# A hybrid decoder trunk: ten in place of six of layer 1's eleven up-projection pairs by seven products, in PSUM chains, with the sums of weights spread over more of the kernel and seven raw buffers

## The chip, the cores and the metric

The kernel runs on one core of one Trainium2 chip. The metric is device time in microseconds (us), the median of three runs. The core has five engines that work side by side: TensorE (PE, matrix products into the PSUM accumulators; its weight loads are listed as PEld), VectorE (DVE), ScalarE (ACT), GpSimd (POOL) and SyncE (SP, which here only issues transfers). Each takes its own instructions in the order in which they were laid down, and waits for others by semaphores.

## What is computed

Two decoder layers over a sequence of 512 rows and 1024 channels. Layer 0 is a causal convolution module, then a feed-forward block; layer 1 is windowed attention, then a feed-forward block; then a last norm. The part that matters here is the feed-forward block of layer 1:

```python
def swiglu_ffn(x, w_up, w_down):
    gate, up = jnp.split(x @ w_up, 2, axis=-1)
    return (jax.nn.silu(gate) * up) @ w_down

h = h + swiglu_ffn(rmsnorm(h, norm_ffn[l]), ffn_w_up[l], ffn_w_down[l])
```

`w_up` is 1024 x 5632 (gate and up), `w_down` is 2816 x 1024.

## The kernel before

**Three matmuls for one product.** A product in float32 accuracy is made of three in a shorter format: every operand is split into a high and a low part, and `mm3` (L352) issues high x high, high x low and low x high (L356 to L358). Weights arrive from memory in chunks of 128 x 1024 (512 KB): `load` (L244) issues the transfer on SP's queue into a tile `raw`, `split_weights` (L272) makes `whi` on ACT (L273) and `wlo` on DVE (L276). `advance` (L278) is called once for each chunk used. It loads up to `DMA_AHEAD` = 6 chunks ahead of the use and splits up to 3 ahead; there are four buffers each of `raw`, `whi` and `wlo`. `PLAN` (L105) is the order of all chunks.

**Pairs.** The 2816 hidden columns of layer 1 are 22 tiles, treated as eleven pairs 0 to 10. A step `("up", p)` computes gate and up of a pair for all 512 rows, a step `("low", p)` multiplies the pairs p and p+1 by their rows of `w_down` and adds to h. `STEPS1` (L32) gives the order: up 0, 1, 2, low 0, then up 3, 4, low 2; up 5, 6, low 4; up 7, 8, low 6; up 9, 10, low 8. Pair 10 is multiplied by its part of `w_down` at the very end, together with the last norm.

**Plain or by seven.** `plain_pair` (L742) uses four chunks and issues 96 matmuls of 512 columns into four PSUM banks. `seven_pair` (L773) cuts the product into 2 x 2 blocks and forms it from seven block products in place of eight (Strassen's scheme in Winograd's form). Each takes one chunk and 24 matmuls of 256 columns into a PSUM bank of its own. Three of the seven use a block of the weights as it is; the others use sums of blocks, S1 to S4. Their partners are blocks of the rows or sums of them, T1 to T4, made once by `Rows.sums` (L723) on POOL and split on ACT and DVE while pair 0 is computed. The results are combined in a tile `c` of four blocks c11 to c22: two copies on ACT (L788, L790), five operations on DVE (L792, L793, L797, L799, L801) and two on POOL (L794, L795). Then come the row scale, silu and the product of gate and up (L807 to L809). `SEVENS` (L57) lists the pairs by seven: 1, 3, 5, 6, 8, 9. So 0, 2, 4, 7 and 10 are plain. All five `low` steps are by seven, and there the products that share a result are added up in one bank already (`CHAINS`, L828): A11, S2, S3, A22 in chain x, S1 and S4 in z, A12 in y. A chain is read after each of its products. For these steps `forms_of` (L814) makes sums of the hidden values on POOL (L823) and splits them on ACT and DVE (L515 to L519).

**The order of the seven.** `SEVEN`, `SEVEN_FIRST` (for pair 1) and `SEVEN_LOW` give three orders; `order_of` picks one.

**Sums of weights.** `prepare` (L252) makes S1 to S4 of each step by seven in device memory: a transfer on SP's queue copies one block (L264), a transfer on POOL's queue adds the other (L268), three sums behind. It is a generator. `advance` takes one step of it at every chunk from the second part of layer 0's feed-forward block on, and it yields twice for a sum, so that a sum is made at every second chunk. The sums are then loaded like any chunk.

**What sets the order.** The kernel is written as a program in one order, and a scheduler lays it out engine by engine with a model of the times. A tile's buffer or PSUM bank (eight banks, L217) is given to a new tile when the last reader of the old one is done. Layer 0 works in two halves of the rows; its first half's projection and the conv of the second half run together. `Next` (L684) and `Rms` (L454) make the norm: squares on ACT, partial sums on POOL (L467), a product with ones on TensorE (L477), the power on POOL (L481), and a spread over the partitions on TensorE (L503). `flip` (L1422) transposes h between the products of pair 1.

Of the kernel before, what the change touches and what calls it, by code (L numbers as in the profile page):

```python
# [18 lines left out]
P = 128  # L19
# [46 lines left out]
def order_of(kind, pair):  # L66
    if kind == "low":
        return SEVEN_LOW
    return SEVEN_FIRST if pair == SEVENS[0] else SEVEN

# [8 lines left out]
def blocks_of(kind, pair):  # L79
    return [(kind, pair, n.split()[0]) for n in order_of(kind, pair)]  # L80

# [118 lines left out]
def hybrid_trunk(ctx: ExitStack, tc: tile.TileContext, xT, W, prm_in, wdw_in, sinks, relb, onehot, fin, lead, out):  # L200
# [33 lines left out]
    summed, preparing, loaded = {}, [iter(())], []  # L234

# [8 lines left out]
    def load(upto):  # L244
        while stream["dma"] < min(len(PLAN), upto):
            i = stream["dma"]
            r = wpool.tile([P, 1024], F32, tag="raw", name=uid("raw"), bufs=4)
            loaded[:] = [nc.sync.dma_start(r, chunk(PLAN[i])).ins]
            raws[i] = r
            stream["dma"] += 1  # L250

    def prepare():  # L252
# [7 lines left out]
        for c in adds + [None] * 3:  # L260
# [8 lines left out]
            yield  # L269
            yield  # L270

# [79 lines left out]

    def mm3(out, w, x, start, stop):  # L352
        if w[1] is None:
            nc.tensor.matmul(out, w[0], x, start=start, stop=stop)  # L354
            return
        nc.tensor.matmul(out, w[0], x[0], start=start, stop=False)  # L356
        nc.tensor.matmul(out, w[0], x[1], start=False, stop=False)  # L357
        nc.tensor.matmul(out, w[1], x[0], start=False, stop=stop)  # L358

# [39 lines left out]

    both = [wpool.tile([P, 1024], F32, tag="raw", name=uid("both"), bufs=4) for _ in range(KT // 2)]  # L400
    x_first = [both[k // 2][:, k % 2 * 512:k % 2 * 512 + 256] for k in range(KT)]
# [308 lines left out]
    class Rows:  # L710
# [12 lines left out]
        def sums(self):  # L723
# [49 lines left out]
    def seven_pair(pair, rows, pool, between=None):  # L773

        c = new_gates(pool)
        c11, c12, c21, c22 = (c[:, m, s] for m in range(2) for s in range(2))
        acc = {}
        for n, name in enumerate(order_of("up", pair)):
            w = [x.rearrange("p (a k c) -> p a k c", a=2, k=4) for x in get_seven("up", pair, n)]
            a, b = name.split()  # L780
            x = rows.block[b]
            r = acc[a] = bank().rearrange("p (a s) -> p a s", a=2)
            for which in range(2):
                for k in range(4):
                    mm3(r[:, which], [v[:, which, k, :] for v in w], [x[e][:, k, :] for e in range(2)],
                        which == 0 and k == 0, which == 1 and k == 3)
            if a == "A11":
                nc.scalar.copy(c11, r)  # L788
            elif a == "S1":
                nc.scalar.copy(c22, r)  # L790
            elif a == "S2":
                nc.vector.tensor_add(c12, r, c11)  # L792
                nc.vector.scalar_tensor_tensor(c21, acc["S3"], -1.0, c12, op0=ALU.mult, op1=ALU.subtract)  # L793
                nc.gpsimd.tensor_add(c12, c12, c22)  # L794
                nc.gpsimd.tensor_sub(c22, c21, c22)  # L795
            elif a == "A12":
                nc.vector.tensor_add(c11, r, c11)  # L797
# [36 lines left out]
    def low_pairs(pair, forms, rs):  # L834

        chains = {}
        for n, name in enumerate(order_of("low", pair)):
            whi, wlo = get_seven("low", pair, n)
# [380 lines left out]

    preparing[0] = prepare()  # L1220
    if True:
# [3 lines left out]
        rate[0] = 2  # L1225

        xkv = x["kv"]
        kq = quads.tile([P, 2, 512], F32, tag="quad", name="kq")
# [199 lines left out]

    forms, signed = {}, None
    for kind, pair in STEPS1:  # L1430
        if kind == "low":
# [77 lines left out]
```

## Time and profile before

| what | value |
|---|---|
| median of 3 runs | 1065.55 us (1065.12 to 1065.77) |
| the profiled execution's own time | 1065.14 us |
| its span, first to last instruction | 1062.6 us |
| mean granted TensorE clock | 0.998 |
| busy: PE / DVE / ACT / POOL | 99% / 70% / 52% / 41% |
| transfers | 187.92 MB, mean 177 GB/s |
| first matmul of pair 1 | 734.07 us |

The span leaves out some 2.5 us around the instructions. The busy share of TensorE counts the modelled ends of overlapping matmuls, so the distance from one start to the next is the better measure of what a matmul costs. In the rows of the profile L12 is line 12 of the kernel, "bank" is a PSUM bank, and the tile in front of the arrow is written, those behind it are read. In the views by time, the number in square brackets is how long the engine stood before the instruction, and for whom.

### The profile page before, as it was taken

Reading aid. Unit: us, or ns where it says so; the run is one execution under the profiler, and the core shown is the slowest. Engines: PE = TensorE matmul, PEld = TensorE weight load, DVE = VectorE, ACT = ScalarE, POOL = GpSimd, SP = SyncE. Lnnn points to the kernel's source line nnn. Section 1 sums busy time; section 2 is a strip of 40 time slices with the busy share of each in tenths; the row PEclk is TensorE's granted clock in tenths of the full one; section 3 lists DMA queues with packets and bytes.
Section 4 is the critical chain, followed back from the end, with each engine's and each line's share of the span. In section 5 each row is a group of like instructions: output and inputs, shape, how many; then the busy total and the mean of one; then the engine's idle time right before and its main releaser. Section 6 shows DMA issues by size and latency. Waiting matters only on the chain.

```text
span 1062.6 us, 16003 instructions
## 1 busy us (share of the span) xinstructions
PE 1051.8 (99%) x5878; PEld 914.9 (86%) x5878; DVE 748.1 (70%) x1159; ACT 554.1 (52%) x968; POOL 433.0 (41%) x523
## 2 busy tenths in 40 slices
PE   9999999999999999999999999999999999999996
PEld 8888889999988888888888877788989899898985
DVE  3999988977776644443437456677778779768867
ACT  3887888864655332322324455465634355444443
POOL 3999998810321311211213254305532415315401
PEclk9999999999999999999999999999999999999999
DMA  9238046576566787677775444466989665455532
GB/s 350 95 96 98 7 139 213 177 226 181 179 182 195 231 209 194 196 187 207 190 206 161 120 140 118 123 177 182 277 248 346 194 186 185 146 159 179 179 119 80
DMA packets 52058, 187.92 MB, mean 177 GB/s; under 512 B 6187, under 2 KB 12492, under 8 KB 51276
## 3 DMA queue, kind: packets, MB, share of 16 engines
q1 hardware_dynamic: 44924, 162.74, 47.5%
q0 software_dynamic: 6336, 23.07, 12.2%
q10 hardware_dynamic: 720, 1.10, 0.3%
q8 instruction: 46, 0.75, 0.3%
q14 instruction: 32, 0.26, 0.1%
HBM read 181.64 MB, written 51.38 MB: 219 GB/s over the span
## 4 chain that ended last, share of the span: by engine, by line
PE 98%; DVE 1%; DMA 1%; ACT 0%; issue 0%; POOL 0%; SPq 0%
PE bank L356 20%; PE bank L358 20%; PE bank L357 20%; PE bank L907 10%; PE bank L849 9%; PE bank L388 5%; PE bank L354 4%; PE bank L389 3%; PE bank L1305 1%; PE bank L1347 1%; PE bank L1334 1%; PE bank L1005 1%; DMA both<-in_lead_dram 1%; PE bank L895 1%; PE bank L1462 0%; PE bank L1426 0%
## 5 line engine op out<-in xcount | busy, mean ns | idle before, releaser
L276 DVE TENSOR_TENSOR wlo<-raw,whi 128x1024 fp32r<-128x1024 f32 x219 | 303.1, 1386 | 169.1 <-ACT whi L273 168.1
L273 ACT CAST whi<-raw 128x1024 fp32r<-128x1024 f32 x219 | 229.7, 1050 | 297.8 <-PE bank L357 189.8
L356 PE MATMUL bank<-quad,whi 128*128 128x512 f32 (+1 forms) x1008 | 349.3, 347 | 0.0
L357 PE MATMUL bank<-quad,whi 128*128 128x512 f32 (+1 forms) x1008 | 348.7, 346 | 0.0
L358 PE MATMUL bank<-quad,wlo 128*128 128x512 f32 (+1 forms) x1008 | 348.3, 346 | 0.0
L356 PEld LDWEIGHTS bank<-quad,whi 128*128 128x128 f32 x1008 | 191.0, 189 | 24.5 <-issue 1.6
L358 PEld LDWEIGHTS bank<-quad,wlo 128*128 128x128 f32 x1008 | 190.9, 189 | 23.6 <-issue 0.6
L357 PEld LDWEIGHTS bank<-quad,whi 128*128 128x128 f32 x1008 | 191.0, 189 | 23.2 <-issue 0.2
L949 POOL TENSOR_TENSOR pr<-pr,pr 128x256 f32<-128x256 f32 x208 | 156.6, 802 | 6.7 <-ACT pr L948 6.7
L956 DVE SCALAR_TENSOR_TENSOR bank<-apad,wdw,bank 128x256 f32<-128x256 f32 x248 | 112.5, 485 | 3.4
L948 ACT ACTIVATE pr<-apad,wdw 128x256 f32<-128x256 f32 x208 | 98.2, 502 | 14.7 <-POOL pr L949 12.7
L907 PE MATMUL bank<-quad,w 128*128 128x256 f32 x448 | 98.7, 380 | 0.0
L907 PEld LDWEIGHTS bank<-quad,w 128*128 128x128 f32 x448 | 84.9, 190 | 11.8 <-DVE bank L956 0.2
L388 PE MATMUL bank<-quad,whi 128*128 128x512 f32 x212 | 75.9, 398 | 0.0
L268 POOL DMA_DIRECT2D sum<-in_W_dram x22 | 18.3, 834 | 117.1 <-DMA sum<-in_W_dram 108.5
L268 POOL DMA_DIRECT2D sum<-sum x22 | 18.0, 819 | 109.6 <-DMA sum<-in_W_dram 104.4
L823 POOL TENSOR_TENSOR up<-up 128x256 f32<-128x256 f32 x40 | 44.1, 1143 | 38.7 <-DVE up L769 37.1
L389 PE MATMUL bank<-quad,wlo 128*128 128x256 f32 x212 | 59.3, 280 | 0.0
L467 POOL TENSOR_TENSOR tmp<-tmp,tmp 128x256 f32<-128x256 f32 (+1 forms) x28 | 27.0, 963 | 78.6 <-ACT tmp L463 62.4
L849 PE MATMUL bank<-wlo,fhi 128*128 128x512 f32 x140 | 55.1, 394 | 0.0
L356 PE MATMUL bank<-rows,whi 128*128 128x256 f32 x192 | 54.6, 285 | 0.0
L358 PE MATMUL bank<-rows,wlo 128*128 128x256 f32 x192 | 54.3, 283 | 0.0
(220 smaller groups left out, 1599.3 us busy)
## 6 DMA issues: line engine op xcount, KB each, us to landing
raw<-in_W_dram SPq DMA_DIRECT2D x187, 512.0 KB, 3.6
sum<-in_W_dram SPq DMA_DIRECT2D x44, 512.0 KB, 5.3
raw<-sum SPq DMA_DIRECT2D x44, 512.0 KB, 3.8
sum<-in_W_dram POOLq DMA_DIRECT2D x22, 512.0 KB, 6.1
sum<-sum POOLq DMA_DIRECT2D x22, 512.0 KB, 6.4
w<-in_W_dram SPq DMA_DIRECT2D x14, 512.0 KB, 8.9
fd<-fs SPq DMA_DIRECT2D x1, 3072.0 KB, 34.5
h<-in_xT_dram SPq DMA_DIRECT2D x8, 256.0 KB, 8.5
```

What stands on the lines that cost most here:

```text
L273: on_act = nc.scalar.copy(hi, src).ins
L276: latest[:] = [on_act, lo_engine[0].tensor_sub(lo, src, f32(hi)).ins]
L356: nc.tensor.matmul(out, w[0], x[0], start=start, stop=False)
L357: nc.tensor.matmul(out, w[0], x[1], start=False, stop=False)
L358: nc.tensor.matmul(out, w[1], x[0], start=False, stop=stop)
L388: nc.tensor.matmul(first[2], first[0], first[1], start=start, stop=False)
L389: nc.tensor.matmul(second[2], second[0], second[1], start=False, stop=stop)
L849: nc.tensor.matmul(out, x, w[:, ws], start=first and e == 0 and i == 0, stop=e == 1 and i == 2, skip_group_check=True)
L907: mm = nc.tensor.matmul(self.pb[:, w * W2:(w + 1) * W2], w1_of(ct, w, k), x[k] if x else xg[k][:, tok], start=k == 0, stop=k == KT - 1)
L948: on_act = nc.scalar.mul(pr, a[:, j:j + W2], tap(j))
L949: on_pool = nc.gpsimd.tensor_add(pr, acc, pr)
L956: on_dve = nc.vector.scalar_tensor_tensor(yt if i == nd - 1 else c, src, tap(i), c if i else self.shift, op0=ALU.mult, op1=ALU.add)
```

## The change

All pairs of layer 1 but pair 0 are computed by seven products (2, 4, 7 and 10 are new). There is one order of the seven for all steps. In `seven_pair` the products of a chain are added up in one PSUM bank, as in the `low` steps, so three banks in place of seven; the combination is four copies on ACT, two of them with the sign turned, and three operations on DVE. T2 is made second, from B22 and T1, and T3 third. `prepare` starts with the second half's projection of layer 0 (`pw2(h1.z, n1)`), and takes a share of a step at each chunk: 1/3, from the second part of the feed-forward block on 1/2, in attention 2/3, in layer 1's feed-forward block 1/4; it yields once for a sum. There are seven `raw` buffers in place of four, and loads run nine chunks ahead in place of six.

```diff
-SEVEN = ("A11 B11", "S3 T3", "S1 T1", "S2 T2", "A12 B21", "S4 B22", "A22 T4")
-SEVENS = (1, 3, 5, 6, 8, 9)
-SEVEN_FIRST = ("A11 B11", "S1 T1", "S3 T3", "S2 T2", "A12 B21", "S4 B22", "A22 T4")
-SEVEN_LOW = ("A11 B11", "S1 T1", "S2 T2", "A12 B21", "S3 T3", "S4 B22", "A22 T4")
+SEVEN = ("A11 B11", "S1 T1", "S2 T2", "A12 B21", "S3 T3", "S4 B22", "A22 T4")
+SEVENS = tuple(range(1, FT // 2))
...
-    DMA_AHEAD, SPLIT_AHEAD = 6, 3
+    DMA_AHEAD, SPLIT_AHEAD = 9, 3
...
-            r = wpool.tile([P, 1024], F32, tag="raw", name=uid("raw"), bufs=4)
+            r = wpool.tile([P, 1024], F32, tag="raw", name=uid("raw"), bufs=7)
...
                 nc.gpsimd.dma_start(summed[a], chunk(a, SUMS[a[2]][1]), accum_op=ALU.add, max_dma_last_dim=4096)
             yield
-            yield
...
-        next(preparing[0], None)
+        share[1] += share[0]
+        while share[1] >= 1:
+            share[1] -= 1
+            next(preparing[0], None)
         load(u + DMA_AHEAD)
...
-            for name, t, f, a, b in (("T1", t1, nc.gpsimd.tensor_sub, b11, b12), ("T3", b12, nc.gpsimd.tensor_sub, b22, b12),
-                                     ("T2", b11, nc.gpsimd.tensor_add, b12, b11), ("T4", b21, nc.gpsimd.tensor_sub, b11, b21)):
+            for name, t, f, a, b in (("T1", t1, nc.gpsimd.tensor_sub, b11, b12), ("T2", b11, nc.gpsimd.tensor_add, b22, t1),
+                                     ("T3", b12, nc.gpsimd.tensor_sub, b22, b12), ("T4", b21, nc.gpsimd.tensor_sub, b11, b21)):
...
-            r = acc[a] = bank().rearrange("p (a s) -> p a s", a=2)
+            x, chain = rows.block[b], CHAINS[a][0]
+            first = chain not in chains
+            if first:
+                chains[chain] = bank().rearrange("p (a s) -> p a s", a=2)
+            r = chains[chain]
...
             if a == "A11":
                 nc.scalar.copy(c11, r)
             elif a == "S1":
-                nc.scalar.copy(c22, r)
+                nc.scalar.mul(c22, r, -1.0)
             elif a == "S2":
-                nc.vector.tensor_add(c12, r, c11)
-                nc.vector.scalar_tensor_tensor(c21, acc["S3"], -1.0, c12, op0=ALU.mult, op1=ALU.subtract)
-                nc.gpsimd.tensor_add(c12, c12, c22)
-                nc.gpsimd.tensor_sub(c22, c21, c22)
+                nc.scalar.copy(c12, r)
             elif a == "A12":
                 nc.vector.tensor_add(c11, r, c11)
+            elif a == "S3":
+                nc.vector.tensor_sub(c22, c22, r)
             elif a == "S4":
                 nc.vector.tensor_add(c12, r, c12)
             elif a == "A22":
-                nc.vector.tensor_sub(c21, c21, r)
+                nc.scalar.mul(c21, r, -1.0)
...
+    preparing[0], share[0] = prepare(), 1 / 3
     n1 = Next(("ffn0",), x0, bc0, HALF[1])
     pw2(h1.z, n1)
...
-    preparing[0] = prepare()
+    share[0] = 1 / 2
     if True:
         ffn_part(0, 1, x0["ffn0"], ALL, Both(), nxt.on_h)
...
+        share[0] = 2 / 3
         xkv = x["kv"]
...
     forms, signed = {}, None
+    share[0] = 1 / 4
     for kind, pair in STEPS1:
```

More of the change, by code (lines that the diff above doesn't have):

```diff
@@ L79, in blocks_of @@
 def blocks_of(kind, pair):
-    return [(kind, pair, n.split()[0]) for n in order_of(kind, pair)]
+    return [(kind, pair, n.split()[0]) for n in SEVEN]
 def is_block(c):
@@ L233, in hybrid_trunk @@
     latest = []
-    summed, preparing, loaded = {}, [iter(())], []
+    summed, preparing, share, loaded = {}, [iter(())], [0, 0], []
     def is_sum(c):
@@ L355, in mm3 @@
             return
-        nc.tensor.matmul(out, w[0], x[0], start=start, stop=False)
-        nc.tensor.matmul(out, w[0], x[1], start=False, stop=False)
-        nc.tensor.matmul(out, w[1], x[0], start=False, stop=stop)
+        nc.tensor.matmul(out, w[0], x[0], start=start, stop=False, **kw)
+        nc.tensor.matmul(out, w[0], x[1], start=False, stop=False, **kw)
+        nc.tensor.matmul(out, w[1], x[0], start=False, stop=stop, **kw)
     class Act:
@@ L398, in hybrid_trunk @@
     w1 = [None] + [quads.tile([P, 2, KT, P], F32, tag="quad", name=uid("w1")) for _ in range(1, KT)]
-    both = [wpool.tile([P, 1024], F32, tag="raw", name=uid("both"), bufs=4) for _ in range(KT // 2)]
+    both = [wpool.tile([P, 1024], F32, tag="raw", name=uid("both"), bufs=7) for _ in range(KT // 2)]
     x_first = [both[k // 2][:, k % 2 * 512:k % 2 * 512 + 256] for k in range(KT)]
@@ L776, in seven_pair @@
         c11, c12, c21, c22 = (c[:, m, s] for m in range(2) for s in range(2))
[L777 to L778 removed]
+        chains = {}
+        for n, name in enumerate(SEVEN):
             w = [x.rearrange("p (a k c) -> p a k c", a=2, k=4) for x in get_seven("up", pair, n)]
             a, b = name.split()
[L781 to L782 removed]
+            x, chain = rows.block[b], CHAINS[a][0]
[3 more added lines that the diff above has]
+            r = chains[chain]
             for which in range(2):
@@ L785, in seven_pair @@
                     mm3(r[:, which], [v[:, which, k, :] for v in w], [x[e][:, k, :] for e in range(2)],
-                        which == 0 and k == 0, which == 1 and k == 3)
+                        first and which == 0 and k == 0, which == 1 and k == 3, skip_group_check=True)
             if a == "A11":
@@ L836, in low_pairs @@
         chains = {}
-        for n, name in enumerate(order_of("low", pair)):
+        for n, name in enumerate(SEVEN):
             whi, wlo = get_seven("low", pair, n)
```

6 lines of the change are left out of this document (1 added, 5 removed).

## The prediction

> **What bounds the kernel now.** I read the page first: the busy shares, then the chain that ended last.
>
> ```profile
> span 1062.6 us, 16003 instructions
> PE 1051.8 (99%) x5878; PEld 914.9 (86%) x5878; DVE 748.1 (70%) x1159; ACT 554.1 (52%) x968; POOL 433.0 (41%) x523
> PE 98%; DVE 1%; DMA 1%; ACT 0%; issue 0%; POOL 0%; SPq 0%
> ```
>
> The reader is to see that TensorE is busy for nearly the whole span and that it alone makes up the chain. A busy TensorE could still be one that is waiting between records, so the next view is that of its waits.
>
> ```profile
> PE bank L441 <- POOL ones_m L438: 1.1, 1, 1.1
> PE bank L895 <- DVE quad L869: 0.7, 2, 0.5
> ```
>
> These are all the waits of TensorE in the execution: three, 1.8 us, all at the very start. In the stage that the change touches it waits for nobody. So time there is won only by giving TensorE less to do, and lost only by making it wait. The third view is the stretch of each pair of layer 1, cut at the first matmul of the pair and the first of what follows.
>
> ```profile
> 758.00:779.88 21.88, 21.88 (x100) 1.00 0.96 276
> 819.30:841.09 21.79, 21.79 (x99) 1.00 0.87 250
> 880.50:900.66 20.16, 20.16 (x170) 1.00 0.59 191
> 941.79:961.95 20.16, 20.16 (x170) 1.00 0.50 151
> 1001.50:1023.29 21.79, 21.79 (x98) 1.00 0.40 130
> ```
>
> The columns are the stretch, its length, TensorE's busy time (with its matmuls, a few of the neighbours among them), granted clock, DMA share and GB/s. Rows 1, 2 and 5 are the plain pairs 2, 4 and 10; rows 3 and 4 are pairs 6 and 8, already by seven products. Both kinds run back to back at clock 1.00. A plain pair is 96 matmuls of 512 columns, so 21.79 / 96 = 0.227 us each. A pair by seven is 7 x 24 = 168 of 256 columns, so 20.16 / 168 = 0.120 us each. The arithmetic falls by an eighth (12.5%), the time only by 7.5%, because the narrow matmul costs more than half of the wide one.
>
> **The change part by part.** *Four more pairs by seven (2, 4, 7, 10).* Pair 7 is mixed with its neighbour in time; I take 21.79 for it too. Removed: 21.88 + 3 x 21.79 = 87.25 us. Added: 4 x 20.16 = 80.64 us. Difference: 6.61 us, all on the chain, since nothing else bounds this stage.
>
> The Trainium skill, "TensorE: Matmul & The Clock Gate", section "Back-to-back issue gap", gives a warm gap of N/2.4 + 2.5 ns, that is 215.8 and 109.2 ns for 512 and 256 columns. By it the saving would be an estimated 96 x 215.8 - 168 x 109.2 = 2.37 us a pair, 9.5 us in all. The trace differs (0.227 and 0.120 us), and it decides.
>
> *What feeds these pairs.* Each takes seven chunks in place of four: 12 more loads, ACT casts and DVE subtractions. Their prices, and those of the evictions that change:
>
> ```profile
> L276 DVE TENSOR_TENSOR wlo<-raw,whi 128x1024 fp32r<-128x1024 f32 x219 | 303.1, 1386 | 169.1 <-ACT whi L273 168.1
> L273 ACT CAST whi<-raw 128x1024 fp32r<-128x1024 f32 x219 | 229.7, 1050 | 297.8 <-PE bank L357 189.8
> L788 ACT COPY up<-bank 128x512 f32<-128x512 f32 x6 | 3.5, 576 | 0.0
> L797 DVE TENSOR_TENSOR up<-bank,up 128x512 f32<-128x512 f32 x6 | 4.1, 687 | 1.0 <-PE bank L358 1.0
> L794 POOL TENSOR_TENSOR up<-up 128x512 f32<-128x512 f32 x6 | 12.0, 2004 | 55.2 <-DVE up L793 55.2
> 880.40:900.50 20.10, 20.10 (x170) 20.10 (x169) 18.08 (x18) 11.16 (x14) 12.63 (x9) 1.00 0.60 193
> 780.00:800.00 20.00, 20.00 (x102) 17.05 (x101) 18.71 (x18) 9.13 (x10) 9.76 (x9) 1.00 0.89 273
> ```
>
> In the last two rows the columns after the stretch are busy PE, PEld, DVE, ACT and POOL. A pair by seven gives DVE 18.08 us of work in 20.10. The change takes two of its evictions of 0.69 us away, so 16.7; ACT gets two more copies of 0.58 (11.16 + 1.15 = 12.3); POOL loses its two additions of about 2 us (12.63 to some 8.8). The down step (last row) has DVE at 18.71 in 20. Up, up, down is then 2 x 16.7 + 18.7 = 52.1 us of DVE in about 60: busy, not the bound. And the sequence has been seen: pairs 5 and 6, both by seven with the dearer evictions, and the down step behind them, ran with no wait of TensorE. I cost the splits and evictions at nothing; TensorE hides them. Without that cover the splits alone would be 12 x 1.386 = 16.6 us of DVE.
>
> *Chains in PSUM.* Products A11, S2, S3 and A22 now add up in one bank, S1 and S4 in another. This adds a wait: S2 may not start before ACT has copied A11's result, S3 not before ACT has copied S2's, A22 not before DVE has read S3's. In between lies one product each time, 20.16 / 7 = 2.88 us. Behind the waiting matmul stands all of TensorE. What the reads take now:
>
> ```profile
> 869.07 1.05 ACT L273 CAST whi<-raw 128x1024 fp32r<-128x1024 f32 x1 [1.83 <-PE bank L357]
> 870.02 0.58 ACT L790 COPY up<-bank 128x512 f32<-128x512 f32 x1
> 884.49 0.58 ACT L788 COPY up<-bank 128x512 f32<-128x512 f32 x1
> 888.09 0.42 ACT L515 ACTIVATE fhi<-up 128x256 fp32r<-128x256 f32 x1 [3.02 <-POOL up L823]
> 946.55 0.57 ACT L788 COPY up<-bank 128x512 f32<-128x512 f32 x1
> ```
>
> Inside a pair, the cast waits for the end of a product and the copy stands behind it: it is done 870.60 - 869.07 = 1.53 us after that end. At the start of pair 6 the A11 product ends at 880.50 + 2.88 = 883.38 and its copy at 885.07, 1.69 us after. At pair 8 it ends at 944.67 and the copy at 947.12, 2.45 us after. All under 2.88, so the wait costs between nothing and what a later copy would bring; I take nothing, the value of the three rows, and keep the late copy as a rival.
>
> *Order of the sums of rows.* T2 is now needed second, not third, and T3 later. Here are the end of T2's split and the first matmul of pair 1:
>
> ```profile
> 731.14 1.21 DVE L516 SCALAR_TENSOR_TENSOR rows<-quad,rows 128x1024 fp32r<-128x1024 f32 x1
> 734.07 0.68 PE L356 MATMUL bank<-quad,whi 128*128 128x256 f32 x1
> ```
>
> T2 is ready before the pair begins, in any place of its order: nothing.
>
> *Sums of weights.* There are 15 steps by seven in place of 11, so 60 sums, not 44: 16 more copies on SP's queue and 16 more additions on POOL's. Before, a sum was made at every second chunk from the first layer's second part on: about 18 + 10 there and in attention, 16 in layer 1. Now: 38 chunks / 3 = 12 in the second half's projection, 36 / 2 = 18, 20 x 2/3 = 13, and 17 left for layer 1 at every fourth chunk.
>
> ```profile
> 231.00:345.00 114.00, 114.00 (x768) 104.86 (x767) 87.33 (x114) 65.74 (x105) 20.66 (x18) 1.00 0.60 185
> 796.00:820.00 24.00, 24.00 (x187) 23.25 (x186) 18.82 (x21) 11.74 (x15) 5.28 (x5) 1.00 1.04 348
> sum<-in_W_dram SPq DMA_DIRECT2D x44, 512.0 KB, 5.3
> sum<-in_W_dram POOLq DMA_DIRECT2D x22, 512.0 KB, 6.1
> POOL sum L268 <- DMA sum<-in_W_dram: 212.9, 34, 12.6
> L264 SPq DMA_DIRECT2D sum<-in_W_dram x44: 494/495/1112, 355.8 to 816.9; - x44
> SPq L248 <- DVE wlo L276: 685.8, 196, 13.1
> 278.10 3.65 POOL L467 TENSOR_TENSOR tmp<-tmp,tmp 128x256 f32<-128x256 f32 x4 [8.35 <-issue]
> 284.98 0.34 PE bank L477 x4
> ```
>
> The new stage (first row) moves 185 GB/s. A sum moves 2 x 0.524 MB; one in 3 x 3.0 us adds 117, so 302 GB/s. The second row is a stretch of layer 1 that moved 348 with TensorE unbroken. In layer 1 it is now four loads and one sum in 11.5 us, 3.15 MB, 274 GB/s: less than the 348 it bears now. Transfers cost nothing while they stay below that. Of the seven raw buffers and nine chunks ahead I expect no gain: TensorE waits for no load today. They double the lead of a load (about six products in place of three). The copies stand in SP's queue among the loads of chunks, 0.5 us of issue each (fifth row); SP spends 685.8 us waiting for a buffer that DVE still reads (sixth), so they fit in between. POOL's additions now stand in a stage of 114 us in which it is busy for 20.66.
>
> **Sum.** The profiled execution took 1065.14 us: a span of 1062.6 and 2.5 around it. 1065.14 - 6.61 = 1058.53. The median of the runs shown is 0.41 above that execution, so 1058.9 us, 0.6% less than 1065.55. What a measurement here can tell from no change is about 0.2%, 2.1 us.
>
> **Rivals.** *Late copy, slower.* Place: the five seams where a pair by seven follows another (1-2, 3-4, 5-6, 7-8, 9-10), of which only 5-6 was there before. ACT runs in order, and at the seam it stands for POOL's sums of the pair before (3.02 us in the row at 888.09), with two casts behind that. If the copy of A11 or S2 is put behind it, TensorE waits. Break-even is 6.61 / 5 = 1.3 us a seam. Were both copies caught, at 3.02 us each with none of their slack left, a seam costs 6.04: 1058.9 + 30.2 = 1089. With one caught in full, 3.02 a seam: 1058.9 + 15.1 = 1074.0, the time I give this rival. For it: pair 8 has only 0.43 us left. Against it: at the one seam of this kind in the trace, 5-6, the copy had 1.19 us left. A mild form, 0.3 to 0.8 us a seam, gives 1060.4 to 1062.9.
>
> *POOL held by an early sum.* POOL too runs in order, and it stood up to 12.6 us for the copy of a sum. In the new stage it makes the partial sums of squares that TensorE takes at 284.98; they end at 281.75, 3.2 us ahead. One landing of 5.3 us in the wrong place costs 2.1 us (1061.0); the longest wait 9.4 (1068.3). Against it: the same mixture ran later in the first layer without a wait of TensorE.
>
> *No narrow-matmul penalty.* If the new pairs paid exactly half for a matmul of half the columns, they would save an eighth of 21.8, 2.7 us each: 1054.6, toward the gap formula above. Every pair by seven in the trace speaks against it.
>
> *The change does nothing.* If the added sums or splits eat what the four pairs give, or the pairs are not shortened: 1065.
>
> **How the numbers follow.** Forecast 1058.9 (1057.5 to 1060.0): 0.66. Mild late copy: 0.12. Late copy in full: 0.08. POOL held: 0.07, most of it near 1061. No penalty: 0.02. Nothing: 0.05. The range from 1056.5 to 1064.0 holds the forecast, the mild copy and most of POOL, about 0.84. Faster by over 0.2% (below 1063.4): 0.85; within 0.2%: 0.06; slower (above 1067.7): 0.09.
>
> **What the profile after would show.** Right: no new row of TensorE's waits, ten pairs of 20.2 us, 16 more sums, DVE below 90% in the pairs, the stage from 734 us on shorter by 6.6 us and the rest unmoved. Wrong: waits of a matmul of L356 for ACT's copies of c11 or c12 at the seams; a wait of L477 for POOL near 285 us; a raw load that a cast waits for; or a pair by seven that takes other than 20.2 us without a wait, by which the price of the matmul, not a wait, would be the failed step.

## The result, and the profile after

| | median, us | runs | ratio to before, 95% interval |
|---|---|---|---|
| before | 1065.47 (1064.09 to 1067.26) | 20 | |
| after | 1063.79 (1059.60 to 1069.28) | 20 | 0.9986 [0.9973, 1.0000] |

The change gives 1.7 us where 6.6 was forecast, at the edge of what a measurement can tell. (Here and below the ratio takes in all runs of both kernels, and the kernel before ran anew beside each experiment, with medians from 1065.09 to 1066.20 us; so it is not the quotient of two medians shown here.) Its runs are also spread over 9.7 us, those of before over 3.2. So not only the middle has to be explained: something in the changed kernel goes well in one run and badly in the next.

The profiled execution after took 1064.78 us. First its page (span and busy shares, then the engines on the chain that ended last):

```profile
span 1063.0 us, 16669 instructions
PE 1047.4 (99%) x6166; PEld 924.3 (87%) x6166; DVE 745.4 (70%) x1163; ACT 576.6 (54%) x1008; POOL 441.4 (42%) x535
PE 87%; ACT 4%; issue 2%; POOL 2%; DVE 2%; DMA 1%; SPq 0%; ACTq 0%; POOLq 0%
```

TensorE is busy for 4.4 us less (1051.8 before), yet the span is not shorter: it now waits. Its waits (total, times, longest):

```profile
PE bank L351 <- DVE wlo L266: 3.5, 1, 3.5
PE bank L434 <- POOL ones_m L431: 1.1, 1, 1.1
PE bank L890 <- DVE quad L864: 1.0, 2, 0.7
PE bank L349 <- ACT up L788: 0.4, 1, 0.4
PE bank L496 <- ACT tmp L482: 0.3, 1, 0.3
```

The second and third stand at the very start, as before. The fourth is a chain in PSUM that waited for ACT's copy: 0.4 us, once. The fifth is a small one in a norm. The first is new: one stop of 3.5 us behind the subtraction that makes `wlo`. Stretches of layer 1 (length; busy PE, PEld, DVE, ACT, POOL; clock, DMA share, GB/s):

```profile
735.00:773.00 38.00, 38.00 (x322) 38.00 (x321) 27.46 (x28) 26.57 (x39) 13.95 (x13) 1.00 0.77 241
800.00:835.00 35.00, 34.65 (x285) 34.22 (x284) 24.62 (x26) 20.02 (x26) 9.50 (x9) 1.00 0.86 259
860.00:895.50 35.50, 35.50 (x297) 35.49 (x296) 25.32 (x27) 20.71 (x27) 9.35 (x9) 1.00 0.94 277
915.00:925.00 10.00, 6.51 (x30) 5.45 (x28) 8.86 (x8) 2.19 (x4) 4.35 (x5) 0.83 0.54 150
925.00:960.50 35.50, 35.50 (x297) 35.50 (x296) 25.00 (x27) 20.78 (x27) 6.88 (x6) 1.00 0.51 168
984.70:1020.20 35.50, 35.50 (x297) 35.50 (x296) 25.01 (x27) 20.79 (x27) 6.88 (x6) 1.00 0.53 171
920.20:923.61 3.41, 3.41 (x13) 2.83 (x12) 3.08 (x4) 0.00 (x0) 0.00 (x0) 0.50 0.58 201
```

Rows 1, 2, 3, 5 and 6 lie in the five places where two pairs by seven follow one another (1 and 2, 3 and 4, up to 9 and 10), without the few matmuls that overlap the down steps. In rows 3, 5 and 6 that is 35.50 / 297 = 0.120 us a matmul, TensorE unbroken, DVE at 70%. Row 2 holds the one stop of a chain, 0.35 us. So the four new pairs, 2, 4, 7 and 10, run at the forecast price. Row 4 is the damage: TensorE is busy for 6.51 of 10 us, and the clock is 0.83. The last row lies inside it. The engines at that place, by time (start, duration; in brackets the idle time before):

```profile
911.99 6.85 DVE L266 TENSOR_TENSOR wlo<-raw,whi 128x1024 fp32r<-128x1024 f32 x1
...
911.83 0.80 POOL L259 DMA_DIRECT2D sum<-sum  x1 [7.99 <-DMA sum<-in_W_dram]
912.39 1.54 POOL L804 TENSOR_TENSOR up<-up 128x512 f32<-128x512 f32 x1
913.65 2.75 POOL L851 TENSOR_TENSOR h<-h,tmp 128x512 f32<-128x512 f32 x2
916.13 3.30 POOL L818 TENSOR_TENSOR up<-up 128x256 f32<-128x256 f32 x3
...
905.33 0.49 SPq L255 DMA_DIRECT2D sum<-in_W_dram  x1
...
915.13 0.28 PE L350 MATMUL bank<-quad,whi 128*128 128x256 f32 x1
918.90 0.39 PE L351 MATMUL bank<-quad,wlo 128*128 128x256 f32 x1 [3.48 <-DVE wlo L266]
```

Read from SP's row up. SP issues the copy of a sum at 905.33. POOL, in its order, stands 7.99 us for the landing, then issues the addition at 911.83. The gate products, the h additions and the sums of hidden values (L818) that had piled up behind come in one burst of six operations, the first five without a gap. DVE's subtraction starts into it and takes 6.85 us; the median of this line in layer 1 is 1.22. TensorE stops from 915.13 to 918.90, and from 920.20 to 923.61 it runs at half the clock (last row of the stretches). The same matmuls take 4.70 us in an unbroken run (shown below); here 915.02 to 925.00, so 5.3 us are lost in one place.

And GpSimd's waits, with those of before (213 us, 34 times) in mind:

```profile
POOL sum L259 <- DMA sum<-in_W_dram: 311.1, 51, 31.6
```

It stands in front of landings for 311 us. The program lets an addition follow three sums behind its copy. But in the trace each of the 60 additions starts 4.7 to 10.6 us after its own copy, the one shown 6.5 us after (905.33 to 911.83): the scheduler has moved it forward to where its copy has only just been issued.

**Theory:** the 6.6 us on TensorE are real, and stops that vary from run to run eat them: GpSimd, held by a landing, is late with small operations that TensorE needs, or does its work in a burst that shuts VectorE out. **Rivals:** the PSUM chains wait; the seven buffers or the traffic disturb the loads; the four pairs give nothing.

### The profile page after: what moved, and what is told of

The parts are those of the page before. It is cut to its first block, busy times and chain, and to the rows that moved or that the text cites. A ratio compares the mean times of both kernels' runs of the same rounds, so it can differ in the third digit from the quotient of the medians.

```text
span 1063.0 us, 16669 instructions
## 1 busy us (share of the span) xinstructions
PE 1047.4 (99%) x6166; PEld 924.3 (87%) x6166; DVE 745.4 (70%) x1163; ACT 576.6 (54%) x1008; POOL 441.4 (42%) x535
## 4 chain that ended last, share of the span: by engine, by line
PE 87%; ACT 4%; issue 2%; POOL 2%; DVE 2%; DMA 1%; SPq 0%; ACTq 0%; POOLq 0%
PE bank L349 19%; PE bank L351 19%; PE bank L350 19%; PE bank L844 9%; PE bank L902 7%; PE bank L381 5%; PE bank L382 3%; ACT pr L943 2%; PE bank L1302 1%; PE bank L1344 1%; PE bank L1331 1%; POOL pr L944 1%; DMA sum<-in_W_dram 1%; DVE wlo L266 1%; DMA both<-in_lead_dram 1%
## 5 line engine op out<-in xcount | busy, mean ns | idle before, releaser
L266 DVE TENSOR_TENSOR wlo<-raw,whi 128x1024 fp32r<-128x1024 f32 x231 | 311.0, 1355 | 160.1 <-ACT whi L263 159.5
L263 ACT CAST whi<-raw 128x1024 fp32r<-128x1024 f32 x231 | 241.0, 1049 | 274.3 <-PE bank L350 189.5
L351 PE MATMUL bank<-quad,wlo 128*128 128x256 f32 (+1 forms) x976 | 326.2, 334 | 3.5 <-DVE wlo L266 3.5
L349 PE MATMUL bank<-quad,whi 128*128 128x256 f32 (+1 forms) x976 | 327.0, 336 | 0.0
L350 PE MATMUL bank<-quad,whi 128*128 128x256 f32 (+1 forms) x976 | 326.1, 334 | 0.0
L349 PEld LDWEIGHTS bank<-quad,whi 128*128 128x128 f32 x976 | 185.5, 190 | 19.8 <-issue 1.6
L350 PEld LDWEIGHTS bank<-quad,whi 128*128 128x128 f32 x976 | 185.5, 190 | 18.5 <-issue 0.2
L349 PE MATMUL bank<-rows,whi 128*128 128x256 f32 x320 | 90.8, 284 | 0.4 <-ACT up L788 0.4
L351 PE MATMUL bank<-rows,wlo 128*128 128x256 f32 x320 | 90.5, 283 | 0.0
L350 PE MATMUL bank<-rows,whi 128*128 128x256 f32 x320 | 90.5, 283 | 0.0
L804 POOL TENSOR_TENSOR up<-up 128x512 f32<-128x512 f32 x20 | 35.6, 1782 | 126.2 <-ACT up L803 126.2
L259 POOL DMA_DIRECT2D sum<-sum x30 | 24.9, 830 | 128.4 <-DMA sum<-in_W_dram 119.2
L349 PEld LDWEIGHTS bank<-rows,whi 128*128 128x128 f32 x320 | 61.4, 192 | 0.8 <-ACT up L788 0.6
L350 PEld LDWEIGHTS bank<-rows,whi 128*128 128x128 f32 x320 | 61.4, 192 | 0.3
```

Source lines behind the costliest of these rows:

```text
L259: nc.gpsimd.dma_start(summed[a], chunk(a, SUMS[a[2]][1]), accum_op=ALU.add, max_dma_last_dim=4096)
L263: on_act = nc.scalar.copy(hi, src).ins
L266: latest[:] = [on_act, lo_engine[0].tensor_sub(lo, src, f32(hi)).ins]
L349: nc.tensor.matmul(out, w[0], x[0], start=start, stop=False, **kw)
L350: nc.tensor.matmul(out, w[0], x[1], start=False, stop=False, **kw)
L351: nc.tensor.matmul(out, w[1], x[0], start=False, stop=stop, **kw)
```

## The experiments

Each edit is against the kernel after, unless said otherwise.

**e3: four pairs plain again.**

```diff
-SEVENS = tuple(range(1, FT // 2))
+SEVENS = (1, 3, 5, 6, 8, 9)
```

> The changed kernel with pairs 2, 4, 7 and 10 plain again: chains, order, spread of the sums and seven raw buffers as changed. If the four pairs by seven are worth 6.6 us of TensorE and the waits are what eats them, this one has no gain to lose: 1065 to 1066 us without waits, up to 1070 if the sums hold POOL here too. If the four pairs are worth nothing on TensorE, it equals the changed kernel, 1062 to 1065, waits included.

Measured: 1065.81 us (1065.13 to 1069.85), ratio 1.0013 [1.0004, 1.0022]. The four pairs are worth something, and the rest of the change is a small loss. With four pairs plain there are also only 44 sums again, the last addition at 703 us, so this takes away 16 sums with the pairs.

**e2: a PSUM bank for each product**, with the combination on DVE and POOL as before.

```diff
-            r = chains[chain]
+            r = acc[a] = bank().rearrange("p (a s) -> p a s", a=2)
...
-                nc.scalar.copy(c12, r)
+                nc.vector.tensor_add(c12, r, c11)
```

> The changed kernel, but each of the seven products of a pair has a PSUM bank of its own again, with the combination on DVE and POOL as it was before; ten pairs, spread and buffers as changed. Theory (POOL held by a sum): the sums stand where they stood, POOL has 3.7 us more of work in each pair, so the time stays at 1062 to 1068 with a wide spread. Rival (late evictions of the chains): no chain is left in the pairs, the time falls to 1058 to 1060.

Measured: 1062.37 us (1058.60 to 1066.25), 0.9975 [0.9962, 0.9988]; against the kernel after this is no clear difference, and the spread is as wide. TensorE's waits:

```profile
PE bank L382 <- DVE wlo L266: 2.1, 2, 1.1
PE bank L843 <- DVE wlo L266: 1.1, 2, 0.6
```

Without the chains there are stops of the same kind, behind the same subtraction, now at other places (330 to 357 us and 846 to 853 us). The chains are not what took the gain.

**e4: four raw buffers, six chunks ahead.**

```diff
-    DMA_AHEAD, SPLIT_AHEAD = 9, 3
+    DMA_AHEAD, SPLIT_AHEAD = 6, 3
...
-            r = wpool.tile([P, 1024], F32, tag="raw", name=uid("raw"), bufs=7)
+            r = wpool.tile([P, 1024], F32, tag="raw", name=uid("raw"), bufs=4)
```

> The changed kernel with four raw buffers and loads six chunks ahead, as before. Theory (POOL held by a sum): the copies of the sums stand closer to their use on SP's queue, the holds differ in place; 1062 to 1068 with a wide spread. If the buffers are what keeps the loads in time, it is slower than the changed kernel by 2 us or more, with casts that wait for a raw load. If the buffers are what hurts, because SP runs further ahead and moves the sums to worse places, it is faster: 1058 to 1061.

Measured: 1062.84 us (1060.44 to 1069.09), 0.9978 [0.9963, 0.9993]: as the kernel after, spread and all. The buffers neither give nor take.

**e1: the sums earlier**, so that none is left for layer 1.

```diff
-    preparing[0], share[0] = prepare(), 1 / 3
+    preparing[0], share[0] = prepare(), 1 / 2
...
-    share[0] = 1 / 2
+    share[0] = 3 / 4
...
-        share[0] = 2 / 3
+        share[0] = 1
```

> The changed kernel with shares of 1/2, 3/4 and 1 in place of 1/3, 1/2 and 2/3, so that all 60 sums of weights are made before layer 1's feed-forward block; nothing else differs. Theory (POOL is held by a sum, does its work in a burst afterwards, and the burst keeps DVE's weight subtraction from its second input): with no sum in that block no subtraction lasts beyond some 2.3 us, TensorE doesn't wait there, the time is 1058 to 1060 us with a spread of 2 us. Rival (the evictions of the PSUM chains are late): the time stays at 1062 to 1066 with the same spread of some 10 us. Rival (the transfers of the sums crowd out the loads): the new crowd is in the first layer and attention, TensorE waits there, and the time is 1062 or more.

Measured: 1063.89 us (1062.42 to 1066.21), 0.9990 [0.9982, 0.9999]. The stops in layer 1 are gone, but pair 1 begins 7 us later. Waits of TensorE, GpSimd by time, and the stretch:

```profile
PE bank L496 <- ACT tmp L482: 4.2, 2, 3.9
```

```profile
289.71 0.81 POOL L259 DMA_DIRECT2D sum<-sum  x1 [3.91 <-DMA sum<-in_W_dram]
290.28 0.99 POOL L474 TENSOR_TENSOR rs<-ms,mhalf 128x2 f32<-128x2 f32 x1
```

```profile
270.00:286.00 16.00, 16.00 (x110) 14.70 (x108) 13.68 (x15) 8.46 (x14) 7.88 (x8) 1.00 1.05 336
286.00:296.00 10.00, 6.08 (x26) 5.02 (x25) 3.95 (x7) 3.57 (x9) 3.19 (x3) 0.71 1.01 309
```

POOL stands 3.91 us for a landing. Behind it waits the power of the norm (L474, two columns), which ACT and then TensorE need. TensorE stops for 4 us and the clock drops to 0.71 over the stretch (0.50 from 290.29 to 297.11). The same fault in another place, the one that the second rival of the prediction had named. The first row shows that 336 GB/s alone did not stop TensorE.

**e5: the sums late and dense**, none in the second half's projection, almost all before layer 1.

```diff
-    preparing[0], share[0] = prepare(), 1 / 3
+    preparing[0], share[0] = prepare(), 0
...
-    share[0] = 1 / 2
+    share[0] = 1
...
-        share[0] = 2 / 3
+        share[0] = 4 / 3
```

> The changed kernel with the sums of weights moved: none in the second half's projection and its layer (share 0 instead of 1/3), then one at every use of the first layer's second part (share 1), 4/3 in the stage behind it and 1/4 in layer 1 as before, so that nearly all of the 60 are done when layer 1 begins. Theory (GpSimd held in its order by a sum's landing, once early in front of the small operations of the normalization, once late in layer 1): no stop of TensorE at 285 to 292 us and none in layer 1 that ends with the subtraction of the low weights; median 1058.5 to 1061.5 us, spread under 4 us. Rival (the gain goes to the PSUM chains or to something else that does not depend on when sums run): 1063 to 1065 us as the changed kernel. Rival (the transfers are now too dense: a sum at each use takes the DMA queues in the first layer's second part): a stop there with DMA as its cause, 1062 us or more.

Measured: 1061.81 us (1060.17 to 1065.14), 0.9965 [0.9951, 0.9978]. By the ratio that is a little over half of the forecast gain. Both named stops are gone, but GpSimd still stands for 204 us in front of landings, and in the profiled run (1064.39 us) TensorE waits for it once in attention (L1331, 1.1 us) and once in the norm in front of it (L470, 0.9 us). Behind the stop of 0.9 us the clock is at half for 3.4 us:

```profile
571.64:575.05 3.41, 3.41 (x19) 3.41 (x18) 3.41 (x6) 0.00 (x0) 1.63 (x2) 0.50 0.77 138
```

Moving the sums moves the fault.

**e6: no sums at all.** The four sums of a unit are each loaded from the block that the sum would start from, so the output leaves the sums out.

```diff
-        return summed[c] if is_sum(c) else W[CHUNK_AT[c]]
+        return W[CHUNK_AT[c[:2] + (SUMS[c[2]][0],) if is_sum(c) else c]]
...
-    preparing[0], share[0] = prepare(), 1 / 3
+    share[0] = 0
```

> The changed kernel with no sums of weights at all: neither copies nor additions; the four blocks of sums in each unit are loaded from the block that the sum would start from, so the outputs leave the sums of weights out and everything that TensorE, VectorE and ScalarE do is the same. Theory (the sums take the gain): 1057.5 to 1060 us, the forecast's 1058.9 in the middle, and runs within 3 us of one another; TensorE waits under 1 us in all. Rival (the stalls come from the chains, the evictions or the split of the added blocks): 1062 us or more, with the same stops in layer 1.

Measured: 1058.43 us (1058.12 to 1058.65), 0.9927 [0.9916, 0.9939]. This is the forecast within half a microsecond, with a spread of 0.5 us. The chains, the buffers and the ten pairs are all in it. The sums cost the whole difference.

**e7: the copies, but no additions.**

```diff
-                nc.gpsimd.dma_start(summed[a], chunk(a, SUMS[a[2]][1]), accum_op=ALU.add, max_dma_last_dim=4096)
```

> The changed kernel with SyncE's copies of the blocks kept and GpSimd's additions left out (so each sum holds its first block alone: the second addend is left out). Theory (what hurts is GpSimd standing in its order in front of an addition whose copy has not landed): as without any sums, 1057.5 to 1060.5 us, no stop. Rival (what hurts is the traffic of 60 more transfers, which delays blocks): the copies are half of the traffic, so about half of the loss is still there, 1061 to 1063 us, and the waits that end TensorE's stops are DMA.

Measured: 1058.48 us (1057.53 to 1059.58), 0.9926 [0.9913, 0.9939]. SP's 60 copies cost nothing. It is the additions, on GpSimd's queue.

**e8: the kernel of e6, with bursts on GpSimd**: five additions of 128x512 behind the A12 addition of every low step.

```diff
+                    if t == 1:
+                        for _ in range(5):
+                            nc.gpsimd.tensor_add(scratch[1], m, scratch[0])
```

> The kernel without sums (sums of weights left out) with one thing put back by hand: five more GpSimd additions of 128x512 with two inputs in SBUF (about 1.3 us each, results unused) back to back in every low step of layer 1, behind the addition of the A12 product: 11 bursts of some 7 to 11 us. Theory (GpSimd's back-to-back reads of SBUF hold VectorE's subtraction of the low weights, 1.2 us alone and 6.85 us beside such a burst at 911.99 us of the changed kernel): subtractions of 3 to 7 us in most of the low steps, TensorE stops of 1 to 4 us each that end with this subtraction, 1068 to 1100 us. Rival (the long subtraction at 912 us was held by the transfers or by something else, not by GpSimd's work): subtractions stay at 1.2 to 1.4 us and the time within 1 us of the kernel without sums, as GpSimd has nothing else urgent here.

Measured: 1060.41 us (1060.05 to 1061.23), 0.9948 [0.9936, 0.9960]; 2.0 us over e6, far under the expected 1068. (There are five low steps, so five bursts; the expectation counted eleven.) TensorE's waits and the subtraction in layer 1 (minimum, median, maximum in ns):

```profile
PE bank L351 <- DVE wlo L266: 0.8, 3, 0.3
```

```profile
L266 DVE TENSOR_TENSOR wlo<-raw,whi x106: 1208/1220/2339, 731.3 to 1038.7; 128x1024 fp32r<-128x1024 f32 x106
```

```profile
856.17 3.54 DVE L266 TENSOR_TENSOR wlo<-raw,whi 128x1024 fp32r<-128x1024 f32 x2
```

Beside such a burst two subtractions in a row (last row, by time) take 3.54 us, 1.77 each, and the longest single one in this stage takes 2.34, while POOL's 25 additions (L860) take 1.29 to 2.37 us: both engines are slowed and neither is shut out. A burst alone does not make 6.85 us. As stated, that part of the theory fell, and the trace of the changed kernel showed what was still missing: an issue of a transfer just ahead of the burst.

**e11: e8 with one issue in front of each burst**, a 512 KB accumulating transfer that waits for nothing.

```diff
+                        with tc.issue_after(added):
+                            added = nc.gpsimd.dma_start(spare[0], W[0], accum_op=ALU.add, max_dma_last_dim=4096).ins
                         for _ in range(5):
-                            nc.gpsimd.tensor_add(scratch[1], m, scratch[0])
+                            with tc.issue_after(added):
+                                nc.gpsimd.tensor_add(scratch[1], m, scratch[0])
```

> The kernel with the bursts of five two-input additions on GpSimd (sums of weights left out) and one more thing: in front of each burst GpSimd issues one 512 KB accumulating transfer that waits for nothing. Theory (a subtraction on VectorE that starts beside GpSimd's issue of a transfer and is followed by a back-to-back burst is shut out of SBUF until the burst ends, as at 911.99 us of the changed kernel: 6.85 us instead of 1.2): single subtractions of 4 to 8 us, TensorE stops of 1 to 4 us in most of the low steps, 1064 to 1080 us. Rival (the issue changes nothing): subtractions up to 1.8 us as in the kernel with bursts alone, 1060 to 1061.5 us.

Measured: 1064.19 us (1063.28 to 1064.74), 0.9987 [0.9978, 0.9996]; 3.8 us over e8. The same two views:

```profile
PE bank L351 <- DVE wlo L266: 4.2, 3, 1.4
```

```profile
L266 DVE TENSOR_TENSOR wlo<-raw,whi x106: 1208/1219/4627, 731.0 to 1041.7; 128x1024 fp32r<-128x1024 f32 x106
```

```profile
855.81 6.87 DVE L266 TENSOR_TENSOR wlo<-raw,whi 128x1024 fp32r<-128x1024 f32 x2
```

And GpSimd's burst, first in e8 (two rows), then in e11:

```profile
855.66 1.29 POOL L860 TENSOR_TENSOR scr<-tmp,scr 128x512 f32<-128x512 f32 x1
856.91 1.72 POOL L818 TENSOR_TENSOR up<-up 128x256 f32<-128x256 f32 x1
...
855.27 0.82 POOL L862 DMA_DIRECT2D sum<-in_W_dram  x1
855.84 1.56 POOL L865 TENSOR_TENSOR scr<-tmp,scr 128x512 f32<-128x512 f32 x1
857.10 0.99 POOL L818 TENSOR_TENSOR up<-up 128x256 f32<-128x256 f32 x1
```

The two subtractions at that place now take 6.87 us together, the longest single one 4.63, and the three stops of TensorE grow from 0.3 to 1.4 us: the low end of what was expected, in three of the five low steps. The order of GpSimd's work at this place is that of e8, so the issue, or the transfer that it starts, makes the difference; the two were not tried apart. In the other two low steps no subtraction starts just behind the issue, and none is held so long. What the records show of the hold stands in the last section.

**e9: the additions held in GpSimd's order.** The program records the latest GpSimd instruction that it has written, and an addition is laid down behind that one, no earlier. `behind[0]` is that instruction.

```diff
-                nc.gpsimd.dma_start(summed[a], chunk(a, SUMS[a[2]][1]), accum_op=ALU.add, max_dma_last_dim=4096)
+                with tc.issue_after(behind[0]):
+                    nc.gpsimd.dma_start(summed[a], chunk(a, SUMS[a[2]][1]), accum_op=ALU.add, max_dma_last_dim=4096)
```

> The changed kernel with each sum's addition on GpSimd held, in the order of its engine, behind the GpSimd instruction that the program writes just ahead of it (in the changed kernel the scheduling layer moved every addition forward to where its own copy had only been issued, so that in its trace each of the 60 starts 4.7 to 10.6 us after its copy, and GpSimd stands still for 311 us in 51 waits for landings). Copies, shares, chains and buffers stay. Theory (GpSimd standing in front of a landing takes the gain): GpSimd's waits for landings fall from 311 us to under 60 us, no stop of TensorE over 0.5 us behind GpSimd's small operations or the subtraction of the low weights, median 1058 to 1060.5 us, spread under 3 us. Rival (the additions cost by their own traffic and by their issue on GpSimd, not by the waiting): 1061 to 1064 us as the changed kernel, though the waits are gone. Rival (the order moves, and a later addition now holds its block): a stop that ends with DMA in layer 1.

Measured: 1059.44 us (1059.03 to 1059.60), 0.9939 [0.9927, 0.9952]. All 60 sums are made, and it is faster than both kernels by more than the intervals. Its five runs lie within 0.6 us of one another. GpSimd's waits for landings, TensorE's waits, and the stretches:

```profile
POOL sum L271 <- DMA sum<-in_W_dram: 13.5, 3, 10.3
...
PE bank L902 <- DVE quad L876: 1.8, 2, 1.4
PE bank L446 <- POOL ones_m L443: 1.1, 1, 1.1
PE bank L508 <- ACT tmp L494: 0.4, 1, 0.4
```

```profile
860.10:895.60 35.50, 35.50 (x297) 35.49 (x296) 25.00 (x27) 20.80 (x27) 8.46 (x8) 1.00 0.94 290
915.10:919.80 4.70, 4.70 (x29) 4.17 (x28) 4.70 (x6) 2.18 (x4) 3.70 (x5) 1.00 0.89 201
919.80:955.30 35.50, 35.50 (x297) 35.48 (x296) 25.02 (x27) 20.81 (x27) 8.48 (x8) 1.00 0.83 244
```

311 us of standing have become 13.5; an addition now starts 21 to 75 us after its copy. TensorE waits only at the start and once for 0.4 us, in a norm. The second row is the place of the big stop (the same end of a down step): 4.70 us in place of 9.98, at clock 1.00. The DMA share in layer 1 is as high as in the kernel after or higher, so the traffic is not what cost.

What the sums still cost can be read by laying the same matmuls of two executions side by side: a product in the first layer, the first matmul of pair 1 and the last matmul, first in e6 (no sums), then in e9, and the last one in the kernel before (its pair 1 begins at 734.07 us):

```profile
172.23 0.50 PE L470 MATMUL bank<-ones_c,tmp 128*128 128x1 f32 x4
733.80 0.68 PE L349 MATMUL bank<-quad,whi 128*128 128x256 f32 x1
1046.75 0.39 PE L1460 MATMUL bank<-whi,hid 128*128 128x512 f32 x1
...
173.27 0.50 PE L482 MATMUL bank<-ones_c,tmp 128*128 128x1 f32 x4
734.98 0.68 PE L361 MATMUL bank<-quad,whi 128*128 128x256 f32 x1
1047.92 0.39 PE L1472 MATMUL bank<-whi,hid 128*128 128x512 f32 x1
...
1053.17 0.39 PE L1462 MATMUL bank<-whi,hid 128*128 128x512 f32 x1
```

In this execution e9 is 1.04 us behind e6 at 173 us, ahead of its first copy (254 us), and 1.17 at the last matmul. From pair 1 on, both take 312.95 us, the kernel before 319.10. So the held sums cost TensorE next to nothing, 0.13 us at most; the rest lies in waits of the first microseconds, where no sum is made.

**e10: the late start of e5 with the additions held** in the same way.

```diff
     preparing[0], share[0] = prepare(), 0
...
+                with tc.issue_after(behind[0]):
```

> The kernel of the late start (sums from the first layer's second part on) with the same hold of the additions behind the GpSimd instruction ahead of them. Theory: as the pinned kernel, 1058 to 1060.5 us; better than the late start alone (1061.81 us, runs 1060.17 to 1065.14), whose additions still wait for 4 to 10 us each. Rival (four transfers per three uses beside the first layer's second part are too dense by themselves): 1061 us or more again.

Measured: 1058.74 us (1057.89 to 1060.21), 0.9934 [0.9922, 0.9947]. As e9: once the additions are held, it hardly matters when the sums are made.

**e12: the same hold in the kernel before.**

```diff
+                with tc.issue_after(behind[0]):
```

> The kernel before with the one edit of the pinned kernel: each sum's addition on GpSimd held behind the GpSimd instruction that the program writes just ahead of it. It tells what the change is worth when the additions of neither kernel stand in front of their landings. Theory (the kernel before lost little to its waits for landings, 213 us of GpSimd's time, since no stop of TensorE in its trace ended with them): 1064 to 1065.5 us, so the change is worth the forecast 5 to 6 us with the additions held in both. Rival (the hold is a gain of its own that has nothing to do with the added sums): 1060 to 1062 us, and the change is worth 1 to 2 us with it as without.

Measured: 1065.35 us (1064.28 to 1067.60), 1.0002 [0.9992, 1.0011], although GpSimd's waits for landings fall from 212.9 to 13.0 us there too. In the kernel before the standing cost nothing. So the change is worth 1065.35 - 1059.44 = 5.9 us when the additions are held in both kernels (6.7 by the two ratios), and 1.7 when they are not.

## Why the prediction was wrong, point by point

- **Four pairs, −6.61 us: right, 0.5 us too large.** 0.120 us a matmul in the unbroken stretches; from pair 1 to the last matmul 319.10 us became 312.95 in e6 and e9, 6.15 less; where the other 0.5 went was not looked into. The price by the gap formula (9.5 us) did not come. That e6 (1058.43 us) and e9 (1059.44) lie so close to the forecast 1058.9 is in part luck: the time around the span, which the sum kept at 2.5 us, is 1.8 in the kernels with ten pairs by seven. Why, no run here shows.
- **Splits and evictions at nothing: right.** DVE is at 70% in the pairs, some 14 us of work for each where 16.7 was reckoned, and where no sum disturbs (e6, and e9 with the sums held) nothing in layer 1 waits for it.
- **Chains at nothing: right** but for 0.4 us (0.8 and 0.3 us in e4). The rival of the late copy, which had the largest chance after the forecast, fell with e2, which has no chains and the same stops, and with e6, which has the chains and the whole gain.
- **Order of the sums of rows at nothing: right.** Pair 1 begins at 734.28 us, 734.07 before.
- **Seven raw buffers, no gain: right** (e4).
- **Sums of weights at nothing: the step that failed.** It weighed bandwidth ("Transfers cost nothing while they stay below that"), and for bandwidth it was right: e7 made all copies and e9 all transfers, and TensorE lost next to nothing. But an addition is also an instruction in GpSimd's order that stands until its copy has landed. The row was quoted, 212.9 us in 34 waits, and read as harmless because TensorE did not wait in that trace. The question that I had to ask of it was what stands behind the waiting addition at each place to which it moves, and how much room that has. In the kernel before there was enough: e12 gains nothing, and three subtractions of 2.55, 3.44 and 3.07 us behind an issue (at 759, 781 and 822 us) stopped TensorE nowhere. The changed kernel has 16 more additions, makes them until 912 us in place of 830, and in the traces some meet work with no room; which of the two counts for more was not tried. From pair 1 on TensorE took 318.82 us in place of 312.95, so 5.9 of the 6.15 us were lost there in the profiled run.
- **The rival "POOL held by an early sum", 0.07: right in its mechanism, mis-sized.** Its price (1061.0 to 1068.3 us) covers 16 of the 20 runs. It was placed at one norm only, at 285 us. There it was a near miss in the profiled run after (GpSimd stood for 1.4 us just in front of the power, L474, and TensorE did not stop), and it struck 4 us later in e1. What spoke against it, "the same mixture ran later in the first layer without a wait", was the trace of a kernel with fewer sums. The second way, a burst behind an issue that shuts out VectorE, the prediction did not have; nor the slow clock behind a stop, 1.6 of the 5.3 us at 915 us (5.28 less a stop of 3.65, which is 3.77 less one step of 0.12).

What is left open: the medians of e9 and e6 differ by 1 us (1059.44 and 1058.43), and their runs do not overlap; in the two profiled executions most of it lies ahead of the sums, but whether it does so in the other runs, and why, was not looked into. Nor was it tried whether a burst that only writes would shut VectorE out too, or whether the transfer behind an issue matters.

## What to carry to other kernels

A transfer that waits for another's landing holds its whole issuing engine; before one is added or moved, list what stands behind it in that engine's order, and keep it so far behind its source that it never waits. Look at the order that the scheduler made, not at the one in the program: the start of each addition less the start of its own copy shows in one column whether the distance survived. And where the runs of a kernel spread over 10 us and those of its neighbours over 3, as here, look for a wait that is decided anew in each run, in several traces: here it was at another place in each variant.

## What the runs showed of the hardware that was not expected

- A VectorE subtraction with two inputs in SBUF, 1.22 us alone, took 1.77 us beside a burst of GpSimd additions (e8; the longest 2.34), up to 4.63 us when the burst followed an issue of a transfer by GpSimd (e11), and 6.85 us in the changed kernel. The Trainium skill, "SBUF — State Buffer", section "Who interferes with whom", says that a VectorE instruction with two SBUF inputs contends with a GpSimd instruction that reads SBUF, for a shared pair of ports that is locked for one of the two. The contention agrees with e8; a delay through five instructions does not follow from it. The single records of GpSimd, whose ends are rough, show a difference: in e8 an operation begins 0.04 us before the one ahead of it has ended (856.91 against 855.66 + 1.29), behind an issue 0.23 to 0.32 us (857.10 against 855.84 + 1.56 in e11). All the traces together hold fourteen subtractions of over 2.5 us that start within 2.4 us behind an issue; each ended 1.1 us after the last of the operations that overlap in this way, in the changed kernel at 918.84, the fifth having ended at 917.75. So the subtraction is let in only where the overlapping row of operations breaks off. Why an issue makes them overlap, no run here shows.
- TensorE's clock fell to half behind three stops, for 3.41 us or twice that. In the changed kernel it was from 920.20 to 923.61, behind the stop of 3.77 us (915.13 to 918.90); in e1 from 290.29 to 297.11, beginning 2.6 us into the stop; in e5 from 571.64 to 575.05, behind a stop of only 0.92 us and eight products of a single column. Half the clock for 3.41 us costs 1.7, so in e5 a small stop cost more by the clock than by its length. The stops of e11 left the clock at 1.00 (view by stretches):

```profile
866.00:874.00 8.00, 6.60 (x55) 6.40 (x54) 7.29 (x7) 2.58 (x3) 0.00 (x0) 1.00 0.57 192
```

Here TensorE stands still for 1.4 of 8 us and keeps its clock. The Trainium skill, "TensorE: Matmul & The Clock Gate", section "What's actually happening", puts the window after which an idle array falls to half rate at about 3.4 us. The length of the slow stretches, 3.41 us and twice 3.41, agrees with such a window; that the array must be idle for all of it does not agree with e5, where a stop of 0.92 us and eight small products were enough, and the measurement decides. So the length of a stop alone does not tell what it costs, and what else decides it, no run here shows.
